# Attention and retention scores on one Trainium2 core: the third part of each score product on 64 or on 128 rows of the array

## The chip, the core and the metric

The kernel runs on one core of one Trainium2 chip. Five engines take part: TensorE (PE in the profile, with its weight loads as PEld), VectorE (DVE), ScalarE (ACT), GpSimd (POOL), and SyncE (SP), which issues the DMAs. Each works through its own queue in order and waits on semaphores for the others. The metric is the device time of one execution in microseconds (us).

## What is computed

A trunk of two layers on 512 tokens of 1024 channels in float32, then a last RMS norm. Each layer normalises x, projects it to all the inputs of three branches, and merges the branches:

```
h = rms_norm(x, norm_g);  proj = h @ w_in
a = diff_attention(aq, ak, av, ...) * silu(az)     # 4 heads, 2 components of 64 dims each
c = short_conv(cx, cb, cc, conv_w) * silu(cz)
r = retention(rq, rk, rv) * silu(rz)               # 4 heads of 64 dims
x = x + (sum_i sigmoid(gate_i) * (branch_i @ w_branch_i)) @ w_out
```

What matters here are the scores. In the attention each head has two components, and for each of them `q @ k.T` over 64 dims, causal, goes through a softmax. In the retention each head has `q @ k.T` over 64 dims with a decay, without a softmax.

## The kernel before

Float32 products are made from parts: a value is split into a high part `hi` (rounded to fp32r) and a low part `lo`, and a product is `hi*hi + hi*lo + lo*hi`. The helper `mm3` issues these three as three products of TensorE. Weights stream in as chunks of 512 KB (`wraw`), which ScalarE casts to `whi` (line 183), and VectorE and GpSimd subtract to `wlo` (line 180), one half of the chunk each. The projections (`proj`) are 24 products of 512 columns, into the PSUM tile `pj`.

Queries and keys have only 64 dims, so two parts fit on the 128 partitions. `queries` makes a tile `st` for each head (or component) `c` with the high part on one half of the partitions (`H[c]`) and the low part on the other. `keys` makes a tile with the key's high part on both halves. One product of the two carries `hi*hi + lo*hi`. The third part is the query's high part times the key's low part. Its operands are the 64 partitions `H[c]` of the query tile and of a tile `lo`, in which the two heads of a pair share the 128 partitions:

```
lo = tr("qk", 10)
for c in range(2):
    V.tensor_tensor(lo[H[c]], y[H[c]], st[H[c]], op=ALU.subtract)
    out.append((st, lo[H[c]]))
```

So each score tile takes two products: one of 128 rows, one of 64 rows. `mm_qk` (line 451) issues them. In an attention step (`attn_step`, one tile of 128 queries against 128, 256, 384 or 512 keys) it has two score tiles, one for each component, and issues the two full-height products first and then the two half-height ones, which lie in different rows of the array. In a retention step (`retention_step`, 128 keys against 512, 384, 256 or 128 queries) there is one score tile, so one full-height and one half-height product. There are 16 steps of each kind in a layer: 64 + 32 products, 192 in both layers.

The order of TensorE's queue is written out by hand. Projections are cut into ticks of 12 products, and `at(lag, fn)` puts a part of a step a few ticks after the part it depends on. Scores are followed by their softmax or mask on VectorE and ScalarE, and the weights (`st`) come back to TensorE as the operands of the value products, some ticks later. The other engines' instructions are put in order by a scheduler when the program is built.

At the start of a layer `Rms.add` squares the eight tiles of x on ScalarE (line 309, tile `sq`, one buffer) and sums them up on GpSimd (line 315, tile `e`). Seven such sums follow one another. Then `Rms.column` sums over the partitions with products on TensorE (line 323), which stand in TensorE's queue between the third and the fourth quarter of the value projection.

Of the kernel before, what the change touches and what calls it, by code (L numbers as in the profile page):

```python
# [10 lines left out]
F32 = mybir.dt.float32  # L11
# [4 lines left out]
PSUM = bass.MemoryType.PSUM  # L16
DRAM = bass.MemoryType.DRAM

P = 128
# [10 lines left out]

# Column offsets of the input projection.
AQ, AK, AV, AZ = 0, 512, 1024, 1536
# [3 lines left out]

# Columns of the small-parameter array.
PG, PCONV, PSUB, PFIN, PW = 0, 16, 40, 42, 50


# [1 line left out]
def merge_chunks(br, jp):  # L42
# [12 lines left out]
def chunk_order(layer):  # L55
    """Chunks of a layer: ("B", col, c) is 512 columns of w_in with K blocks 2c and
    2c+1; ("A", col) 128 columns with all of K; ("W", br, c) 256 columns of
    w_branch; ("O", c) 128 columns of w_out."""
    L = [("B", c, i) for c in (AV, RV) for i in range(4)]
    L += pair_chunks(AK, AQ, AZ)  # L60
    for i in range(4):
        L += conv_chunks(i)
    L += pair_chunks(AK + 256, AQ + 256, AZ + 256)
    for jp in range(4):
        L += merge_chunks(1, jp)
    L += pair_chunks(RK, RQ)
    for jp in range(4):
        L += [("A", RZ + P * jp)] + merge_chunks(0, jp)
    for jp in range(4):
        L += merge_chunks(2, jp)  # L70
    for _ in range(1 if layer < DEPTH - 1 else 2):
        L += [("O", c) for c in range(8)]
    return L


def rot_perm(base):
    """Column order of a rotation head pair block: the two halves of a pair lie
    16 partitions apart within a block of 32."""
    idx = []
    for h in range(4):  # L80
        for ihi in range(2):
            for half in range(2):
                for ilo in range(16):
                    idx.append(base + h * 64 + half * 32 + ihi * 16 + ilo)
    return idx
# [32 lines left out]
def tables():  # L118
    """Rotation tables (attention, then retention k and q of each head pair, the
    decays folded in) and the constant matrices."""  # L120
    f = np.float32
# [33 lines left out]
def tile_hybrid_trunk(ctx: ExitStack, tc: tile.TileContext, xT, w, prm, lam, tab, cmat, outT):  # L155
# [34 lines left out]

# [1 line left out]
    order = [(l, c) for l in range(DEPTH) for c in chunk_order(l)]  # L192
# [21 lines left out]
    def chunk(l, *key):  # L214
        """Next chunk in parts; the one after it is on its way."""
        assert order[pos[0]] == (l, key), (order[pos[0]], l, key)
        while len(parts) < min(LOOK + 1, len(order) - pos[0]):
            split_next()
        pos[0] += 1
        return parts.pop(0)  # L220

# [1 line left out]
    # Projections are cut into ticks of 12 products. The steps of the attentions,  # L223
    # whose products wait for other engines, are placed between them: each part of
    # a step comes a few ticks after the one it depends on.
    now = [0]
# [14 lines left out]

# [1 line left out]
    par = t("par", 1, (P, PW))  # L243
    nc.sync.dma_start(par, prm)
    eps = t("eps", 1, (P, 1))
    G.memset(eps, EPS)
    # The tensor engine comes up to its clock, and the scalar engine's functions
    # load, while the first tiles arrive.
    warm = t("wb", 1, (P, S), mybir.dt.bfloat16)
# [23 lines left out]
    G.memset(ones_d, 1.0 / D)  # L273
    # -lambda of each layer on every partition, and the sub-norm gains.
    nlam, gsub = [], []
# [18 lines left out]
    xsave = dr.tile([D, S], F32, tag="xsave", bufs=1, name="xsave")  # L294

    MASK8 = [i ^ 8 for i in range(32)]
    MASK16 = [i ^ 16 for i in range(32)]

    class Rms:
        """Statistics of the tiles of x over their channels, for tokens q0 to q1."""  # L300

# [3 lines left out]
        def add(self, xk, end=False):  # L305
            """A tile; the end tile's squares stay apart, for a short way to the sums."""
            n = self.n
            sq = t("e2" if self.acc is None else "sq", 1)
            A.activation(sq[:, :n], xk, AF.Square)
            if self.acc is None:  # L310
                self.acc = sq
            elif end:
                self.end = sq
            else:
                G.tensor_tensor(self.acc[:, :n], self.acc[:, :n], sq[:, :n], op=ALU.add)  # L315

        def column(self):
            """1/rms as a column of each token tile."""
            nt = self.n // P
# [11 lines left out]
        def row(self, col):  # L331
            """1/rms as a row on every partition, in PSUM."""
            row = pa()
            for i in range(self.n // P):
                T.transpose(row[:, i * P:(i + 1) * P], col[:, i:i + 1].broadcast_to([P, P]), ident)
            return row

    ctx.enter_context(tc.manual_schedule(engines={mybir.EngineType.PE}))
    for l in range(DEPTH):
        last = l == DEPTH - 1  # L340
        ng = [par[:, PG + 8 * l + k:PG + 8 * l + k + 1] for k in range(NK)]

# [1 line left out]
        xg = {}  # L344
# [8 lines left out]

# [1 line left out]
        def values(col, banks, cs):  # L355
# [34 lines left out]

# [1 line left out]
        h = []  # L392
# [26 lines left out]

        # Queries and keys of two heads (or components) of 64 dims, stacked on the  # L420
        # partitions so that one product carries hi*hi + lo*hi; the third part
        # multiplies the query's hi rows with the key's lo rows.
        H = [slice(0, 64), slice(64, 128)]

        def queries(o, cs, msk):
            y = rotated(o, cs, msk)
            out = []
            for c in range(2):
                st = tr("qk", 10)
                A.copy(st[H[c]], y[H[c]])  # L430
                V.tensor_tensor(st[H[1 - c]], y[H[c]], st[H[c]], op=ALU.subtract)
                out.append((st, st[H[c]]))
            return out

        def keys(o, cs, msk):
            y = rotated(o, cs, msk)
            lo = tr("qk", 10)
            out = []
            for c in range(2):
                st = tr("qk", 10)  # L440
                A.copy(st[H[c]], y[H[c]])
                A.copy(st[H[1 - c]], y[H[c]])
                V.tensor_tensor(lo[H[c]], y[H[c]], st[H[c]], op=ALU.subtract)
                out.append((st, lo[H[c]]))
            return out

        def mm_qk(outs, a, asl, b, bsl):
            """Two of them; their half-height parts lie in different rows of the array."""
            for i in range(2):
                for o, ac, bc in zip(outs, a, b):  # L450
                    T.matmul(o, ac[i][:, asl], bc[i][:, bsl], start=i == 0, stop=i == 1)  # L451
# [5 lines left out]

        # sigmoid(v) = (1 + tanh(v/2)) / 2, which needs no other table than Exp's; the
        # halves are left to later steps.
        def tanh_half(out, o):  # L460
# [11 lines left out]
        def head_out(o, z, g, out):  # L472
            """Normalised, gated head output in parts; o is [v dim, token], z twice the
            gate and g a factor that takes it back."""
            sq = t("sq", 1)
# [19 lines left out]

# [1 line left out]
        rbr, rz = [], {}  # L497
# [19 lines left out]

# [1 line left out]
        cbr = []  # L519
# [18 lines left out]

# [1 line left out]
        abr, az = [], {}  # L540
        cs_a = table(0)

        def attn_qk(p):
            k2 = [keys(proj(AK + 256 * p + P * i), cs_a, MASK8) for i in range(2)]
            q2 = [queries(proj(AQ + 256 * p + P * i), cs_a, MASK8) for i in range(2)]
            return {2 * p + i: (q2[i], k2[i]) for i in range(2)}

        def attn_step(hd, i, o, wt, qk):
            """Scores and weights of one query tile; every second one, the values."""
            q, k = qk[hd]  # L550
# [50 lines left out]

# [1 line left out]
        m = [None] * NK  # L603
# [35 lines left out]
        for jp in range(4):  # L639
            merge(1, cbr, jp, True, False)  # L640
        rk = sum((keys(proj(RK + P * b), table(1 + 2 * b), MASK16) for b in range(2)), [])
        rq = sum((queries(proj(RQ + P * b), table(2 + 2 * b), MASK16) for b in range(2)), [])
# [9 lines left out]

# [1 line left out]
        x2 = []  # L654
# [6 lines left out]
        def out_proj(q0, q1):  # L661
            """The tiles of the output in turn; the last parts of m come late, so that
            the first two tiles' products with them wait behind the others."""
            ws, os = {}, {}
# [70 lines left out]
```

## Time and profile before

| what | value |
|---|---|
| time, median of 3 runs | 1091.72 us (1090.1 to 1093.24) |
| span of the profiled execution, first to last instruction | 1090.5 us |
| TensorE busy | 1078.6 us, 99% of the span, 5010 products |
| VectorE busy | 676.4 us, 62% |
| ScalarE busy | 504.6 us, 46% |
| GpSimd busy | 329.8 us, 30% |
| mean granted TensorE clock | 0.996 |

The profile is of one execution and gives its span; the times of the runs are given apart from it. Products are pipelined, and the time of one in the profile overlaps the next, so a busy share near 100% doesn't say that each product runs at its shortest. What a product costs is better read from the chain of work that ended last: its pieces lie end to end, each as long as the step from one product's end to the next one's. In the chain, a piece such as `PE pa L451 x4` is four products of line 451 into `pa` in a row.

### The profile page before, as it was taken

Reading aid. Unit: us, or ns where it says so; the run is one execution under the profiler, and the core shown is the slowest. Engines: PE = TensorE matmul, PEld = TensorE weight load, DVE = VectorE, ACT = ScalarE, POOL = GpSimd, SP = SyncE. Lnnn points to the kernel's source line nnn. Section 1 sums busy time; section 2 is a strip of 40 time slices with the busy share of each in tenths; the row PEclk is TensorE's granted clock in tenths of the full one; section 3 lists DMA queues with packets and bytes.
Section 4 is the critical chain, followed back from the end, with each engine's and each line's share of the span. In section 5 each row is a group of like instructions: output and inputs, shape, how many; then the busy total and the mean of one; then the engine's idle time right before and its main releaser. Section 6 shows DMA issues by size and latency. Waiting matters only on the chain.

```text
span 1090.5 us, 13839 instructions
## 1 busy us (share of the span) xinstructions
PE 1078.6 (99%) x5010; PEld 878.1 (81%) x5010; DVE 676.4 (62%) x1158; ACT 504.6 (46%) x944; POOL 329.8 (30%) x258
## 2 busy tenths in 40 slices
PE   8999999999999999999999999999999999999997
PEld 6888888888887778888888878888788877788896
DVE  6787686755676556444438766868546946654344
ACT  6454453543554445333444535445344635543343
POOL 6222223221232232323532212232123223232264
PEclk9999999999999999999999999999999999999999
DMA  6322222232234122434422232223212322124353
GB/s 232 117 96 97 78 77 82 94 116 79 77 116 136 58 78 78 135 129 129 158 87 97 86 109 78 78 82 124 85 59 97 135 97 73 62 97 132 111 197 123
DMA packets 34340, 113.64 MB, mean 104 GB/s; under 512 B 3936, under 2 KB 3936, under 8 KB 34272
## 3 DMA queue, kind: packets, MB, share of 16 engines
q1 hardware_dynamic: 34272, 112.76, 30.2%
q8 instruction: 39, 0.64, 0.2%
q14 instruction: 29, 0.24, 0.1%
HBM read 108.55 MB, written 4.19 MB: 103 GB/s over the span
## 4 chain that ended last, share of the span: by engine, by line
PE 97%; POOL 1%; DMA 1%; ACT 0%; DVE 0%; issue 0%; SPq 0%; DVEq 0%; POOLq 0%; ACTq 0%
PE pj L187 29%; PE pj L189 28%; PE pj L188 28%; PE pa L451 3%; PE pa L187 3%; PE pa L188 2%; PE pa L189 2%; PE pa L577 1%; POOL e L315 1%; DMA wraw<-w 1%; PE pa L485 0%; PE pa L484 0%; POOL wlo L180 0%; DVE p L693 0%; PE pa L323 0%
## 5 line engine op out<-in xcount | busy, mean ns | idle before, releaser
L180 POOL TENSOR_TENSOR wlo<-wraw,whi 128x512 fp32r<-128x512 f32 x184 | 252.6, 1375 | 640.4 <-ACT whi L183 619.0
L187 PE MATMUL pj<-h,whi 128*128 128x512 f32 x960 | 384.6, 401 | 0.0
L188 PE MATMUL pj<-h,whi 128*128 128x512 f32 x960 | 375.9, 392 | 0.0
L189 PE MATMUL pj<-h,wlo 128*128 128x512 f32 x960 | 375.7, 391 | 0.0
L183 ACT CAST whi<-wraw 128x512 fp32r<-128x512 f32 x368 | 217.1, 617 | 241.3 <-PE pj L188 178.9
L180 DVE TENSOR_TENSOR wlo<-wraw,whi 128x512 fp32r<-128x512 f32 x184 | 152.9, 832 | 131.7 <-ACT whi L183 128.3
L189 PEld LDWEIGHTS pj<-h,wlo 128*128 128x128 f32 x960 | 180.2, 188 | 41.3
L187 PEld LDWEIGHTS pj<-h,whi 128*128 128x128 f32 x960 | 180.4, 188 | 40.5 <-issue 1.7
L188 PEld LDWEIGHTS pj<-h,whi 128*128 128x128 f32 x960 | 180.6, 188 | 35.2
L187 PE MATMUL pj<-xb,whi 128*128 128x512 f32 x192 | 76.3, 397 | 0.0
L189 PE MATMUL pj<-xb,wlo 128*128 128x512 f32 x192 | 75.3, 392 | 0.0
L188 PE MATMUL pj<-xb,whi 128*128 128x512 f32 x192 | 75.0, 390 | 0.0
L564 ACT ACTIVATE p<-pa,nm 128x128 f32<-128x128 f32 (+3 forms) x64 | 33.4, 525 | 70.5 <-DVE nm L561 70.0
L488 DVE RECIPROCAL e<-e 128x512 f32<-128x512 f32 x16 | 53.6, 3351 | 18.1 <-ACT e L487 18.1
L183 ACT CAST st<-pa 128x256 fp32r<-128x256 f32 (+2 forms) x80 | 29.7, 372 | 74.7 <-DVE pa L506 43.1
L187 PE MATMUL pj<-vm,whi 128*128 128x256 f32 (+1 forms) x192 | 61.0, 318 | 0.0
L189 PE MATMUL pj<-vm,wlo 128*128 128x256 f32 (+1 forms) x192 | 60.7, 316 | 0.0
L188 PE MATMUL pj<-vm,whi 128*128 128x256 f32 (+1 forms) x192 | 60.6, 316 | 0.0
L621 DVE SCALAR_TENSOR_TENSOR wb<-wa,pj 128x512 f32<-128x512 f32 x32 | 22.0, 688 | 44.9 <-PE pj L189 44.9
L451 PE MATMUL pa<-qk 128*128 128x256 f32 (+3 forms) x192 | 46.5, 360 | 0.0
L451 PEld LDWEIGHTS pa<-qk 128*128 128x128 f32 x192 | 29.8, 185 | 19.1 <-issue 13.6
L180 DVE TENSOR_TENSOR st<-pa,st 128x256 fp32r<-128x256 f32 (+2 forms) x80 | 33.7, 421 | 18.4 <-ACT st L183 18.2
(123 smaller groups left out, 1414.7 us busy)
## 6 DMA issues: line engine op xcount, KB each, us to landing
wraw<-w SPq DMA_DIRECT2D x183, 512.0 KB, 3.3
tab<-tab SPq DMA_DIRECT2D x10, 512.0 KB, 3.3
xm<-xT SPq DMA_DIRECT2D x16, 256.0 KB, 3.5
xsave<-xm SPq DMA_DIRECT2D x8, 256.0 KB, 2.0
xm<-xsave SPq DMA_DIRECT2D x8, 256.0 KB, 2.7
outT<-p SPq DMA_DIRECT2D x8, 256.0 KB, 2.1
wraw<-w SPq DMA_DIRECT2D x2, 256.0 KB, 3.1
cm<-cmat SPq DMA_DIRECT2D x1, 256.0 KB, 6.6
```

The lines of the kernel that those rows point to most:

```text
L180: eng.tensor_tensor(lo, x, hi, op=ALU.subtract)
L183: A.copy(hi, x)
L187: T.matmul(out, wh, xh, start=start, stop=False)
L188: T.matmul(out, wh, xl, start=False, stop=False)
L189: T.matmul(out, wl, xh, start=False, stop=stop)
L315: G.tensor_tensor(self.acc[:, :n], self.acc[:, :n], sq[:, :n], op=ALU.add)
L451: T.matmul(o, ac[i][:, asl], bc[i][:, bsl], start=i == 0, stop=i == 1)
L488: V.reciprocal(r, r)
L564: A.activation(pc[:, :n], sp[:, :n], AF.Exp, bias=nm, scale=0.125, accum_out=sm)
L577: T.transpose(tp[:, j * P:(j + 1) * P], p1[:, j * P:(j + 1) * P], ident)
L621: V.scalar_tensor_tensor(y, g, 1.0, o, op0=ALU.add, op1=ALU.mult)
```

## The change

The low part of the keys gets four tiles of its own, `klo`, made once, one for each head of the two pairs. In each, one half of the partitions is set to zero by GpSimd at the start and never written again. `keys` writes the low part into the other half, the half `H[c]` on which the query tile has its high part. `queries` and `keys` hand out whole tiles, so the third part is a product of 128 rows whose other half is multiplied by zero. `mm_qk` issues the two products of one score tile one after the other, instead of both first parts and then both third parts. The tag `qk` has 8 buffers instead of 10. (Comments in the file are gone too, and line numbers behind the new lines are shifted: line 451 becomes 453, line 315 becomes 321, line 323 becomes 329.)

```diff
+    H = [slice(0, 64), slice(64, 128)]
+    klo = [tr("klo", 4) for _ in range(4)]
+    for n, lo in enumerate(klo):
+        G.memset(lo[H[1 - n % 2]].bitcast(F32), 0.0)
...
-                st = tr("qk", 10)
+                st = tr("qk", 8)
                 A.copy(st[H[c]], y[H[c]])
                 V.tensor_tensor(st[H[1 - c]], y[H[c]], st[H[c]], op=ALU.subtract)
-                out.append((st, st[H[c]]))
+                out.append((st, st))
...
-        def keys(o, cs, msk):
+        def keys(o, cs, msk, i):
             y = rotated(o, cs, msk)
-            lo = tr("qk", 10)
             out = []
             for c in range(2):
-                st = tr("qk", 10)
+                st, lo = tr("qk", 8), klo[2 * i + c]
                 A.copy(st[H[c]], y[H[c]])
                 A.copy(st[H[1 - c]], y[H[c]])
                 V.tensor_tensor(lo[H[c]], y[H[c]], st[H[c]], op=ALU.subtract)
-                out.append((st, lo[H[c]]))
+                out.append((st, lo))
             return out
 
         def mm_qk(outs, a, asl, b, bsl):
-            """Two of them; their half-height parts lie in different rows of the array."""
-            for i in range(2):
-                for o, ac, bc in zip(outs, a, b):
+            for o, ac, bc in zip(outs, a, b):
+                for i in range(2):
                     T.matmul(o, ac[i][:, asl], bc[i][:, bsl], start=i == 0, stop=i == 1)
...
-            k2 = [keys(proj(AK + 256 * p + P * i), cs_a, MASK8) for i in range(2)]
+            k2 = [keys(proj(AK + 256 * p + P * i), cs_a, MASK8, i) for i in range(2)]
...
-        rk = sum((keys(proj(RK + P * b), table(1 + 2 * b), MASK16) for b in range(2)), [])
+        rk = sum((keys(proj(RK + P * b), table(1 + 2 * b), MASK16, b) for b in range(2)), [])
```

TensorE's queue at the first attention step, before (`pa<-qk` is a score product, `pj<-h,whi` a product of a projection; the size is that of the output):

```order
L188 MATMUL pj<-h,whi 128x512
L189 MATMUL pj<-h,wlo 128x512
L451 MATMUL pa<-qk 128x128 x4
L187 MATMUL pj<-h,whi 128x512
L188 MATMUL pj<-h,whi 128x512
L189 MATMUL pj<-h,wlo 128x512
```

and after:

```order
L188 MATMUL pj<-h,whi 128x512
L189 MATMUL pj<-h,wlo 128x512
L453 MATMUL pa<-qk 128x128
L453 MATMUL pa<-klo,qk 128x128
L453 MATMUL pa<-qk 128x128
L453 MATMUL pa<-klo,qk 128x128
L187 MATMUL pj<-h,whi 128x512
L188 MATMUL pj<-h,whi 128x512
```

The four products of the step stand at the same place between the same projections; the two third parts, now with `klo`, no longer stand side by side.

GpSimd's queue at the start, before (`wlo` is the low part of a weight chunk, `e` the running sum of squares of x, `wu` two zero columns of the convolution):

```order
L273 MEMSET ones_d 128x1
L526 MEMSET wu 128x2
L180 ISA
L180 TENSOR_TENSOR wlo<-wraw,whi 128x512
L315 TENSOR_TENSOR e_222<-e_222,sq 128x512
L180 TENSOR_TENSOR wlo<-wraw,whi 128x512
L315 TENSOR_TENSOR e_222<-e_222,sq 128x512 x2
L180 TENSOR_TENSOR wlo<-wraw,whi 128x512
L315 TENSOR_TENSOR e_222<-e_222,sq 128x512 x4
L180 TENSOR_TENSOR wlo<-wraw,whi 128x512 x16
```

and after:

```order
L273 MEMSET ones_d 128x1
L300 MEMSET klo 64x512 x4
L528 MEMSET wu 128x2
L180 ISA
L180 TENSOR_TENSOR wlo<-wraw,whi 128x512 x2
L321 TENSOR_TENSOR e_230<-e_230,sq 128x512 x2
L180 TENSOR_TENSOR wlo<-wraw,whi 128x512
L321 TENSOR_TENSOR e_230<-e_230,sq 128x512 x5
L180 TENSOR_TENSOR wlo<-wraw,whi 128x512 x16
```

Four memsets of `klo` are new, and the first sum of squares has moved behind the low part of the second weight chunk. In the rest of TensorE's queue nothing moves, and on the other engines a few casts and subtractions change places with a neighbour.

## Rows read from the trace of the kernel before

**Rows 1.** The page's head: the span.

```profile
span 1090.5 us, 13839 instructions
```

**Rows 2.** The page's chain that ended last: shares by engine.

```profile
PE 97%; POOL 1%; DMA 1%; ACT 0%; DVE 0%; issue 0%; SPq 0%; DVEq 0%; POOLq 0%; ACTq 0%
```

**Rows 3.** Waits of PE, longest (who <- whom: us, times, longest).

```profile
PE pa L323 <- POOL e L315: 2.5, 1, 2.5
```

**Rows 4.** PE's waits again, of its weight loads: the longest.

```profile
PEld pa L451 <- issue: 13.6, 48, 0.4
```

**Rows 5.** The chain in pieces (start us, length us, what): attention score groups.

```profile
88.91 0.43 PE pa L451 x4
89.33 0.43 PE pj L187
...
97.80 0.55 PE pa L451 x4
...
106.92 0.72 PE pa L451 x4
...
116.34 0.88 PE pa L451 x4
117.22 0.32 PE pa L187
```

**Rows 6.** The chain in pieces: retention score groups.

```profile
337.43 0.65 PE pa L451 x2
338.08 0.43 PE pj L187
...
341.01 0.54 PE pa L451 x2
...
347.94 0.43 PE pa L451 x2
348.36 0.37 PE pa L187
...
351.82 0.31 PE pa L451 x2
```

**Rows 7.** The chain in pieces: full-height products of 512, 256, 128 and 384 columns.

```profile
88.67 0.23 PE pj L189
...
117.54 0.12 PE pa L188
...
130.11 0.44 PE pa L577 x4
...
348.73 0.17 PE pa L188
348.91 0.18 PE pa L189
```

**Rows 8.** POOL in order of time, start (start us, us, line, op, [idle before <-releaser]).

```profile
0.77 0.52 POOL L250 MEMSET wb<- 128x512 bf16 x1
...
6.92 1.30 POOL L180 TENSOR_TENSOR wlo<-wraw,whi 128x512 fp32r<-128x512 f32 x1 [5.56 <-ACT whi L183]
8.17 1.74 POOL L315 TENSOR_TENSOR e<-e,sq 128x512 f32<-128x512 f32 x1
10.60 1.62 POOL L180 TENSOR_TENSOR wlo<-wraw,whi 128x512 fp32r<-128x512 f32 x1 [0.69 <-ACT whi L183]
```

**Rows 9.** The chain in pieces: the last two sums of squares.

```profile
22.13 1.28 POOL e L315
...
24.15 1.29 POOL e L315
```

**Rows 10.** PE by stretch (from:to us, length, busy (products), PEclk, DMA share, GB/s).

```profile
27.40:30.70 3.30, 3.30 (x9) 0.50 0.60 190
```

**Rows 11.** VectorE and PE in order of time at retention's last step.

```profile
420.34 0.28 DVE L180 TENSOR_TENSOR st<-pa,st 128x128 fp32r<-128x128 f32 x1
...
423.05 0.22 PE L187 MATMUL pa<-st,vm 128*128 128x128 f32 x1
```

More of the change, by code (lines that the diff above doesn't have):

```diff
@@ L418, in rotated @@
             return t1
-        H = [slice(0, 64), slice(64, 128)]
         def queries(o, cs, msk):
```

## The prediction

> **What bounds the kernel now.** I read the chain of work that ended last first, then who waited for whom on PE, then the chain piece by piece around the score products. The chain is PE for 97% of a span of 1090.5 us [rows 1, 2]: whatever PE spends on a product is spent on the end time, and whatever another engine spends is free as long as PE does not come to wait for it. PE waits in one place that matters, 2.5 us for POOL's line 315 near the start [rows 3]. So two questions remain: what the 192 score products cost PE in its own queue, and whether the change moves that one wait.
>
> The pieces of the chain lie end to end, so they can be added. A product of 512 columns takes 0.23 us, one of 384 columns 0.17 to 0.18 (0.175 below), one of 256 columns 0.12, and four of 128 columns 0.44, so 0.11 each [rows 7]. All of these use 128 rows. The score groups are dearer, and so is the product that follows them: it takes 0.43 where 0.23 is normal [rows 5, 6]. A group costs its own piece plus the next product's excess over its normal price.
>
> **What the score groups cost today.** Attention, four products per step, two of them of half height: 128 columns 0.43 + 0.43 - 0.23 = 0.63 us; 256 columns 0.55 + 0.20 = 0.75; 384 columns 0.72 + 0.20 = 0.92; 512 columns 0.88, and the product behind it has 256 columns and takes 0.32 instead of 0.12, so 1.08 [rows 5, 7]. Retention, two products per step, one of half height: 512 columns 0.65 + 0.20 = 0.85; 384 columns 0.54 + 0.20 = 0.74; 256 columns 0.43, and the product behind it (384 columns) takes 0.37 instead of 0.175, so 0.625; 128 columns 0.31 + 0.20 = 0.51 [rows 6, 7]. Each of these eight stands eight times in the trace (four heads, two layers); the first stands in the rows, with one 0.43 of the product behind for all.
>
> Take the full-height products off at their normal price and the half-height part remains. At 512 columns it is 1.08 - 0.46 = 0.62 in attention, where there are two half-height products, and 0.85 - 0.23 = 0.62 in retention, where there is one. At 384 columns 0.57 and 0.565, at 256 columns 0.51 and 0.505, at 128 columns 0.41 and 0.40. So two facts are in the rows. The second half-height product of a pair is free: the pair does run side by side. And going to half height and back costs 0.3 to 0.4 us over a product's normal price, every time, with or without a partner. The weight loads of these groups show it too: PE's loader stands idle ahead of them 48 times, 13.6 us in all, with nothing that it waits for [rows 4].
>
> **The change part by part.**
>
> *Half height to full height.* Attention now pays four normal products, retention two. I price them by [rows 7], where full-height products of each width stand between others with no gap. Attention: 0.63 - 0.44 = 0.19; 0.75 - 0.48 = 0.27; 0.92 - 0.70 = 0.22; 1.08 - 0.92 = 0.16; together 0.84, eight times: 6.7 us saved. Retention: 0.85 - 0.46 = 0.39; 0.74 - 0.35 = 0.39; 0.625 - 0.24 = 0.385; 0.51 - 0.22 = 0.29; together 1.46, eight times: 11.7 us saved. Sum: **-18.4 us**, all on PE and so all on the path. Both ends: the gap could go wholly (-18.4) or stay wholly (rival one). I take the first, because no full-height neighbour shows a gap: the four products at 130.11 are narrow, stand alone between 512-column ones, and cost 0.44 [rows 7].
>
> The Trainium skill bears on this from both sides. "TensorEngine Tiling (Array Packing)", section Theoretical Speedup, gives up to 2x for a contraction of 64 rows or fewer, which speaks against this change; its section Key Properties says that a change of tiling mode drains the engine, which speaks for it. The trace agrees with the first only where two half-height products stand together, as 0.62 against 0.62 shows, and has 0.3 to 0.4 us for the second. By the first rule alone the change would lose time (rival one gives that sum); by both it gains what the rows say.
>
> *The order inside a group.* The two products of one score tile now follow each other into the same PSUM bank. The three products of every projection already do that at 0.23 us each. Nothing.
>
> *Four key tiles with a zero half.* POOL gets four memsets of 64x512 near the start. The nearest row is its memset of 128x512 bf16, 0.52 us; as many bytes in one of the new ones, twice that if the 4-byte words count double: 2.1 to 4.2 us for four. POOL is idle for 5.56 us between its last small memset and its first weight part [rows 8]. Hidden; without that cover up to 4.2 us would come ahead of the first weight part. The subtractions into these tiles keep their number and size, and each tile is reused in the same turn as the shared one was.
>
> *POOL's order at the start.* The built order moves something that the diff doesn't mention. Before, the first sum of squares (line 315, at 8.17) runs ahead of the second chunk's weight part, which waits for its data until 10.60 [rows 8]. After, it stands behind that weight part and starts at about 10.60 + 1.62 = 12.2, where the second sum ran before. Every later sum then comes one round later, since each waits for a square that ScalarE writes only when the sum before has read the one buffer. A round is 24.15 - 22.13 = 2.02 us, and the last sum, which ends at 24.15 + 1.29 = 25.44, is what PE waits for [rows 3, 9]. PE's next instruction in its queue is the product with these sums, so all projections behind it wait too: **+2.0 us**, uncovered.
>
> *The clock behind that stall.* After the stall of before, the granted clock stood at 0.50 (the lower level, 1.2 GHz) from 27.4 to 30.7, and PE started 9 products there [rows 10]; at 0.23 each they would be 2.1 us instead of 3.3 to 3.8. PE had stood idle in the stall before the clock fell. A longer stall may bring a second such stretch, up to 1.7 us more; it may also put part of the slow stretch into the stall, a gain of up to 1.7. I take 0 and keep the loss for the range.
>
> *Sum.* 1090.5 - 18.4 + 2.0 = 1074.1 us for the span. The median of the runs, 1091.7, lies 1.2 above the profiled span; with that, **1075.3 us**.
>
> **The rivals.**
>
> *One: the gap isn't the height's.* If the 0.3 to 0.4 us belonged to something that stays (entering the score group, its PSUM banks, the release of its tiles), the change would only give up the free partner: one more product per attention step, (0.11 + 0.12 + 0.175 + 0.23) x 8 = 5.1 us, plus the 2.0 of the start: **1098.8 us**, slower. For it: nothing in the trace shows the same tiles at full height. Against it: the transposes also write a fresh PSUM tile and have no gap [rows 7]. The gaps are 18.4 + 5.1 = 23.5 us in all; the sign turns where less than 7.1 of them go, 30%.
>
> *Two: another engine takes the gain back.* With PE faster, a product may come to wait for VectorE or ScalarE. The tightest step that I found is the last one of retention: VectorE ends the low part at 420.34 + 0.28 = 420.62, and the value products that take it begin on PE at 423.05 [rows 11], 2.4 us to spare; PE loses at most two score groups of 0.39 between such a pair. So I expect no wait. If retention were paced by VectorE after all, its 11.7 us would stay: **1087.0 us**.
>
> *Three: half the gap stays*, for instance on the way into a group but not on the way out: 18.4 - 11.75 = 6.7 gained, less 2.0: **1087.0 us** as well.
>
> **How the numbers follow.** Forecast 0.84; rival one 0.05; rivals two and three together 0.08; no difference, where the gains of three are smaller still and the start costs both terms, 0.03. Two and three count as faster, and 0.3% is 3.3 us, about what a measurement of this kernel can tell from no change. So faster 0.92, same 0.03, slower 0.05. The range: below, no cost at the start, or a shorter slow stretch, with the spread of the runs (1.6 us below the median), 1091.7 - 18.4 - 1.6 = 1071.7; above, the second slow stretch and the runs' 1.5 above the median, 1075.3 + 1.7 + 1.5 = 1078.5, and a microsecond for narrow products that cost more between other neighbours, 1079.5. That leaves out less than 2 in 10.
>
> **What would show it.** In the chain of after: a four-product group of 128 columns at about 0.44, of 512 columns at 0.92, a retention pair of 512 columns at 0.46, and the product behind each back at 0.23 to 0.28. PE's wait for line 321 (315 before) at 4.5 us, ending near 27.5. One slow stretch of the clock behind it, or two. Wrong would be: groups whose piece keeps 0.2 us or more over these prices; a new wait of PE for VectorE in retention; a stall at the start that is no longer than 2.5 us.

## The result and the profile after

The kernel after takes 1076.52 us (median of 4 runs, 1075.94 to 1077.81), the kernel before 1091.94 us: the ratio is 0.9855, 95% interval 0.9843 to 0.9868, about 15.4 us faster. The forecast was 1075.3. The execution that was profiled is the slowest of the four (1077.81 us; its span, which leaves out 1.8 us, is 1076.0), and the lines of after in this section are of that one.

The head of the page of after, and its TensorE clock in 40 slices:

```profile
span 1076.0 us, 13845 instructions
...
PEclk9899999999999999999999999999999999999998
```

The chain is still PE for 97%. What changed is seen in its pieces (start us, length us, what), for the same steps as [rows 5] and [rows 6]. Attention, four products each:

```profile
92.53 0.40 PE pa L453 x4
92.93 0.28 PE pj L187
...
101.23 0.47 PE pa L453 x4
...
110.08 0.69 PE pa L453 x4
...
119.27 0.94 PE pa L453 x4
120.20 0.12 PE pa L187
```

Retention, two products each:

```profile
337.65 0.46 PE pa L453 x2
338.10 0.23 PE pj L187
...
340.87 0.35 PE pa L453 x2
...
347.43 0.23 PE pa L453 x2
347.66 0.18 PE pa L187
...
350.95 0.17 PE pa L453 x2
351.13 0.28 PE pj L187
```

The product behind a group is back at its normal price: 0.23 for 512 columns, 0.12 for 256, 0.18 for 384, where [rows 5, 6] had 0.43, 0.32 and 0.37. Only behind a 128-column group does it take 0.28, and the group is shorter by nearly as much: 0.40 + 0.28 - 0.23 = 0.45 in attention, 0.17 + 0.28 - 0.23 = 0.22 in retention. The idle time of the weight loads in front of the score products [rows 4] no longer stands in the list of waits at all.

Where the rest went is read from PE's wait for the sums of squares, and from the granted clock behind it (PE by stretch: from:to, length, busy (products), PEclk, DMA share, GB/s):

```profile
PE pa L329 <- POOL e L321: 4.4, 1, 4.4
```

```profile
27.80:34.60 6.80, 6.80 (x20) 0.50 0.61 183
```

The wait was 2.5 us before [rows 3], and the clock stood at its lower level (0.50, 1.2 GHz) for some 3.4 us [rows 10]; now it stands there for 6.8.

The two traces can be set against each other at three places. Two of them are the four transposes of the start and the second product behind the last score group, in the chain of before:

```profile
33.70 0.44 PE pa L335 x4
...
951.89 0.24 PE pj L188
...
1083.70 0.42 PE pa L335 x2
```

and in the chain of after:

```profile
37.33 0.44 PE pa L341 x4
...
937.07 0.23 PE pj L188
...
1068.87 0.68 PE pa L341 x2
```

The first stands 3.6 us later than before: so much was lost at the start. The second stands 14.8 ahead, so 18.4 us were gained between the two places, where all score groups lie. The third place is the end, 14.4 ahead (1090.46 and 1076.03, less rounded): another 0.4 went in the last stretch. So -18.4 + 3.6 + 0.4 = -14.4 us, the difference of the two spans.

The third line of each chain shows most of that last loss: the two transposes of the end begin 14.8 ahead as well, and take 0.68 where they took 0.42. In after the clock had fallen just before them, in before it had not yet (PE by stretch, first before, then after):

```profile
1080.00:1085.40 5.40, 2.55 (x21) 1.00 0.00 0
```

```profile
1068.90:1075.90 7.00, 0.63 (x2) 0.50 0.41 151
```

### The profile page after: what moved, and what is told of

Its sections match the earlier page's. It is cut to its first block, busy times and chain, and to the rows that moved or that the text cites. A ratio compares the mean times of both kernels' runs of the same rounds, so it can differ in the third digit from the quotient of the medians.

```text
span 1076.0 us, 13845 instructions
## 1 busy us (share of the span) xinstructions
PE 1062.3 (99%) x5010; PEld 883.2 (82%) x5010; DVE 680.7 (63%) x1158; ACT 504.4 (47%) x944; POOL 331.6 (31%) x262
## 4 chain that ended last, share of the span: by engine, by line
PE 97%; POOL 1%; DMA 1%; ACT 0%; DVE 0%; issue 0%; SPq 0%; DVEq 0%; POOLq 0%; ACTq 0%
PE pj L187 29%; PE pj L189 28%; PE pj L188 28%; PE pa L453 3%; PE pa L189 2%; PE pa L188 2%; PE pa L187 2%; POOL e L321 1%; PE pa L579 1%; DMA wraw<-w 1%; PE pa L487 0%; PE pa L486 0%; POOL wlo L180 0%; PE pa L329 0%; DVE p L695 0%
## 5 line engine op out<-in xcount | busy, mean ns | idle before, releaser
L180 DVE TENSOR_TENSOR wlo<-wraw,whi 128x512 fp32r<-128x512 f32 x184 | 156.3, 850 | 125.0 <-ACT whi L183 121.5
L189 PEld LDWEIGHTS pj<-xb,wlo 128*128 128x128 f32 x192 | 36.0, 188 | 8.4
L188 PEld LDWEIGHTS pj<-xb,whi 128*128 128x128 f32 x192 | 36.1, 188 | 7.9
```

Of the source, the lines that this page charges most:

```text
L180: eng.tensor_tensor(lo, x, hi, op=ALU.subtract)
L188: T.matmul(out, wh, xl, start=False, stop=False)
L189: T.matmul(out, wl, xh, start=False, stop=stop)
```

## The experiments

**The order alone.** The kernel before, with only the two loops of `mm_qk` changed over:

```diff
-            for i in range(2):
-                for o, ac, bc in zip(outs, a, b):
+            for o, ac, bc in zip(outs, a, b):
+                for i in range(2):
```

> The kernel before with the order of after alone: each score tile's full-height product is followed at once by its own half-height one, all third parts still on 64 rows. Theory (each change of height costs 0.3 to 0.4 us, a second half-height product beside the first is free): an attention step now changes height twice, so it pays its half-height part twice: (0.62 + 0.57 + 0.51 + 0.41) x 8 = 16.9 us more than before, about 1108.8 us against 1091.9; an attention group of 512 columns about 1.7 us in the chain instead of 1.08; retention unchanged. Rival one (the gap belongs to the score group and not to the height): only the free partner is lost, 5.1 us, about 1097.

Measured: 1109.68 us (1108.94 to 1110.61) against 1092.4 on the same chip, ratio 1.0154 (1.0137 to 1.0170): 17.3 us slower, where the theory wanted 16.9 and the rival 5.1. The chain of this run, the first four attention steps:

```profile
89.08 0.82 PE pa L451 x4
89.91 0.43 PE pj L187
...
98.36 1.05 PE pa L451 x4
99.41 0.43 PE pj L187
...
107.98 1.28 PE pa L451 x4
109.25 0.43 PE pj L187
...
117.94 1.52 PE pa L451 x4
119.46 0.31 PE pa L187
```

The 512-column step costs 1.52 + 0.31 - 0.12 = 1.71, where it cost 1.08: the half-height part of 0.62 is paid twice. In the program only this order differs, so half the change alone would have made the kernel slower by more than the whole change gains.

**The height alone.** The kernel after, with the loops of before (both first parts, then both third parts):

```diff
-            for o, ac, bc in zip(outs, a, b):
-                for i in range(2):
+            for i in range(2):
+                for o, ac, bc in zip(outs, a, b):
```

> The kernel after with the order of before: both first parts, then both third parts, all on 128 rows. Theory (height alone decides): the same as after, 1076.5 within 1 us, groups at 0.44 to 0.92 us. Rival (two products in a row into the same PSUM tile are what saves the time in attention): attention's 6.7 us come back, about 1083.

Measured: 1076.56 us (1076.14 to 1076.74), the same as after. At full height the order inside a group is worth nothing that these runs can tell; two products in a row into one PSUM tile neither cost nor save.

**The pair twice.** The kernel before, with the two half-height products of an attention step issued a second time behind the first two:

```diff
-                    T.matmul(o, ac[i][:, asl], bc[i][:, bsl], start=i == 0, stop=i == 1)
+                    T.matmul(o, ac[i][:, asl], bc[i][:, bsl], start=i == 0, stop=i == 1 and len(outs) == 1)
+            if len(outs) == 2:
+                for o, ac, bc in zip(outs, a, b):
+                    T.matmul(o, ac[1][:, asl], bc[1][:, bsl], start=False, stop=True)
```

> The kernel before, with the pair of half-height products of each attention step issued twice in a row (the third part is added twice, so the scores are not the reference's). Theory (the cost is in the change of height, not in the product): the second pair costs one product's normal price per step, (0.11 + 0.12 + 0.175 + 0.23) x 8 = 5.1 us, about 1097.0 against 1091.9. Rival (each half-height product or pair carries the 0.3 to 0.4 us itself): 2.11 x 8 = 16.9 us, about 1108.8.

Measured: 1097.37 us (1095.48 to 1098.90) against 1092.4, ratio 1.0043 (1.0031 to 1.0055): 5.0 us, as the theory had it. In the chain the second pair has a piece of its own (line 454):

```profile
89.06 0.43 PE pa L451 x4
89.49 0.11 PE pa L454 x2
89.61 0.43 PE pj L187
...
98.06 0.55 PE pa L451 x4
98.61 0.12 PE pa L454 x2
...
107.31 0.72 PE pa L451 x4
108.03 0.18 PE pa L454 x2
...
116.90 0.89 PE pa L451 x4
117.80 0.23 PE pa L454 x2
```

Two half-height products together take 0.11, 0.12, 0.18 and 0.23, what one full-height product of that width takes [rows 7]. The pair does run side by side at no extra cost; the 0.3 to 0.4 us belong to going in and out, and are paid once whether one product, one pair or two pairs stand between. What they are made of inside the engine, no run here separates.

**Retention alone.** The kernel after, with attention's third part on the halves of the new tiles and its loops as before:

```diff
-                out.append((st, st))
+                out.append((st, st, st[H[c]]))
...
-                out.append((st, lo))
+                out.append((st, lo, lo[H[c]]))
...
-            for o, ac, bc in zip(outs, a, b):
-                for i in range(2):
-                    T.matmul(o, ac[i][:, asl], bc[i][:, bsl], start=i == 0, stop=i == 1)
+            for i in range(2):
+                for o, ac, bc in zip(outs, a, b):
+                    j = 2 if i == 1 and len(outs) == 2 else i
+                    T.matmul(o, ac[j][:, asl], bc[j][:, bsl], start=i == 0, stop=i == 1)
```

> Only retention on 128 rows; attention's third parts stay on 64 rows, side by side, as before, reading the halves of the new tiles. POOL's order at the start is that of after. Theory (a height change costs the same with one half-height product as with two): retention's 11.7 us are gained and the start costs 2.0 to 3.6, so about 1082 to 1084 against 1091.9. Rival (the cost goes with the number of half-height products, of which retention has 64 of 192 score products' 96 third parts, a third): 23.5 / 3 less retention's own slots, about 6 us gained at most, 1088 to 1090.

Measured: 1083.73 us (1083.33 to 1084.05) against 1092.4, ratio 0.9916 (0.9901 to 0.9930): 8.7 us faster, which is 11.7 less 3.0 for the start; in the chain of this run the four transposes of the start stand at 36.80, 3.1 later than before. Attention then brings 1083.73 - 1076.56 = 7.2, where 6.7 was forecast. Retention, with one third of the score products, brings most of the gain, because its half-height product had no partner.

**The start: the memsets on VectorE.**

```diff
-        G.memset(lo[H[1 - n % 2]].bitcast(F32), 0.0)
+        V.memset(lo[H[1 - n % 2]].bitcast(F32), 0.0)
```

> The kernel after with the four memsets on VectorE instead of GpSimd; with that the built order of GpSimd's and ScalarE's start is that of before again (the first sum of squares ahead of the second chunk's weight part). Theory (the moved sum costs one round of 2.0 us of stall and up to one slow stretch of the clock, 1.6): 2.0 to 3.6 us less than after, 1073 to 1074.5 against 1076.5; PE's wait for the sums back from 4.4 to 2.5 us, one slow stretch of 3.4 us. Rival (the start is hidden behind something later): 1076.5.

Measured: 1073.78 us (1072.15 to 1074.05), ratio to before 0.9822 (0.9809 to 0.9836), beside the kernel after itself on the same chip:

> The kernel after once more, beside the two on the same chip: 1076.5 within 1 us, both theories.

which took 1076.49 us (1075.12 to 1076.78), ratio 0.9848 (0.9834 to 0.9861). So 2.7 us are back, the clock's part included. GpSimd's order is that of before, and PE's wait is 2.0 us, near the 2.5 of before. The profiled execution shows one thing more. It took 1072.15 us, the shortest of its four runs, and in it the clock never fell at the start (the wait, then PE by stretch):

```profile
PE pa L329 <- POOL e L321: 2.0, 1, 2.0
```

```profile
23.00:25.30 2.30, 0.35 (x2) 1.00 0.00 0
25.40:27.30 1.90, 1.90 (x13) 1.00 0.04 9
27.40:30.70 3.30, 3.30 (x17) 1.00 0.61 179
```

17 products start between 27.4 and 30.7 where [rows 10] has 9. The three other runs of the same kernel took 1073.6 to 1074.05. One stretch at the lower level is worth about 8 products x 0.2 = 1.6 us, which is also the distance of this run to the others; their traces were not taken, so that they had such a stretch is inferred. Their mean granted clocks agree with it: 0.996, 0.995 and 0.995 against 0.998, and 3.4 us at half the clock are 0.0016 of the span.

**The start: two tiles for the squares.** As above, and the squares alternate between `sq` and `wc`:

```diff
-            sq = t("e2" if self.acc is None else "sq", 1)
+            self.i += 1
+            sq = t("e2" if self.acc is None else ("sq", "wc")[self.i % 2], 1)
```

> The same, and the squares of x alternate between two tiles (the convolution's tile wc is the second), so that a square needn't wait for the sum before it. Theory (the round of 2.0 us is the two engines waiting for each other through one buffer): seven sums of 1.3 to 1.7 us with two weight parts between them end by about 22 to 23 us, where PE is still busy until 23; no wait of PE for the sums, no slow stretch, another 2.5 + 1.6 us gained, 1069 to 1070.5. Rival (the scaled tiles of x, which now stand behind squares on ScalarE, come late for PE instead): a new wait of PE of 1 to 3 us near the start, 1072 to 1074.

Measured: 1073.73 us (1073.09 to 1074.01), the same as with the memsets on VectorE alone. The theory failed, and the rival was right on the time and on a new wait of 1 to 3 us. It had half of the cause: PE no longer waits for the sums, but for VectorE's low part of the next weight chunk, not for a scaled tile of x. The chain of this run leads from that low part back through VectorE to a scaled tile that ScalarE makes late, behind a square (first the wait, then the chain):

```profile
PE pj L188 <- DVE wlo L180: 2.0, 1, 2.0
```

```profile
20.12 0.49 ACT sq L316
...
20.94 0.63 ACT xb L356
...
21.60 1.78 DVE xb L357
...
25.64 0.61 DVE wlo L180
```

The clock falls behind this stall as it did behind the other (PE by stretch):

```profile
27.10:30.40 3.30, 3.30 (x9) 0.50 0.75 205
```

**The start: four tiles for the squares.** With the memsets on VectorE, and the squares in the four tiles of `ez`:

```diff
-            sq = t("e2" if self.acc is None else "sq", 1)
+            sq = t("e2", 1) if self.acc is None else t("ez", 4)
```

> As the run with two square tiles, but the squares rotate through the four tiles of the tag ez (gates of heads, unused at the start), so that ScalarE doesn't stand still before a square and the scaled tiles of x behind it come early too. Theory (the start's stall is the engines waiting for each other through too few square tiles, first at the sums, then, with two tiles, at VectorE's low part of the last weight chunk, because ScalarE's scaled tiles of x came late): no wait of PE between 6 and 34 us above 0.5, no slow stretch, 2.0 to 2.5 + up to 1.6 us less than with the memsets on VectorE alone, 1069.5 to 1072 against 1073.8. Rival (GpSimd's sums and VectorE's subtractions slow one another and the last low part stays late): a wait of 1 to 2 us at the same place, 1073 to 1074.

Measured: 1071.98 us (1071.39 to 1073.66) against 1093.35 in that call, ratio 0.9814 (0.9800 to 0.9828), the best median of the study, but its interval overlaps those of the two runs before it (0.9809 and 0.9810 to 0.9836). The first line below is PE's wait, the next two are pieces of the chain behind it, the others VectorE in order of time:

```profile
PE pj L188 <- DVE wlo L180: 1.4, 1, 1.4
```

```profile
27.35 0.23 PE pj L189
...
30.75 0.23 PE pj L189
```

```profile
17.31 1.78 DVE L356 SCALAR_TENSOR_TENSOR xb<-xm,par,xb 128x512 fp32r<-128x512 f32 x1
...
24.52 0.74 DVE L356 SCALAR_TENSOR_TENSOR xb<-xm,par,xb 128x512 fp32r<-128x512 f32 x1
...
25.43 0.68 DVE L180 TENSOR_TENSOR wlo<-wraw,whi 128x512 fp32r<-128x512 f32 x1
```

The same operation takes 1.78 us at 17.31, while GpSimd makes a weight part and adds squares, and 0.74 at 24.52, where GpSimd stands idle from 24.58 on. VectorE reaches the low part that PE waits for only at 25.43. PE's products behind the wait stay at 0.23 us, so the clock did not fall in this execution. The theory's "no wait above 0.5" failed and the rival holds in part: the wait shrank from 2.0 to 1.4, and didn't go. That GpSimd's work is what slows VectorE is read from one trace side by side; no run separated it. What might remove the wait (VectorE's lambda work out of the start, or less on GpSimd) wasn't tried.

By the clocks on record, most of the lead in the median is the clock's. Three of the five runs have a mean granted clock of 0.997 to 0.998 and took 1071.4 to 1072.0; the other two (0.995, 0.996) took 1073.3 and 1073.7. With the memsets alone only one run of four had 0.998. Among runs of like clock, four square tiles are about half a microsecond ahead, which is little beside the spread. Why the clock fell less often is not shown.

## Why the prediction was right

*The score groups, -18.4 us.* Right in sum and in its parts. The chain of after has nearly the prices that were taken: 0.45, 0.47, 0.69 and 0.94 in attention against 0.44, 0.48, 0.70 and 0.92, and 0.46, 0.35, 0.23 and 0.22 in retention against 0.46, 0.35, 0.24 and 0.22. Between the two marks 18.4 us were gained. That the gap goes with the change of height, which the trace of before only suggested, is shown by the first and the third experiment: one more change of height per attention step costs 17.3 us, one more pair without a change costs 5.0.

*Rival one* (the gap belongs to the score group) falls with the same two runs, and with the second: the same groups, tiles and order at full height have no gap. The Trainium skill's page "TensorEngine Tiling (Array Packing)" gives both halves of this in its sections Theoretical Speedup and Key Properties: up to two products of 64 rows in the time of one, and a drain of the engine at a change of mode. The traces agree with the first, with 0.23 us for a pair of 512 columns; for the second they show a cost, 0.3 to 0.4 us for going in and out, and not the drain itself. That the second outweighs the first here is this kernel's: only one pair, or one product, stood between two changes.

*The four memsets, hidden.* Right: they took 2.2 us together, near the lower bound, in GpSimd's idle stretch, of which 3.2 us are left.

*The moved sum, +2.0 us.* Right: the wait grew from 2.5 to 4.4, and undoing GpSimd's order gave 2.7 back, the clock's part included. Reading the built order, not the diff, brought this term.

*The clock, taken at 0.* This is the term that was mis-sized. Of the 3.6 us lost at the start 2.0 are the moved sum, and 1.6 the lower level, which held for 6.8 us instead of 3.4; that is within the bound of 1.7 that was kept for the range. In the second trace of the same kernel the four transposes stand at 36.67, with PE's wait ending at 27.24, and the clock cost 1.2: there the fall came inside the stall, as the prediction had thought possible. The 0.4 of the last stretch was no term of the sum; 0.26 of it is the clock again, at the two last transposes.

*The total, and some luck.* Span against span, the sum gave 1074.1 and the profiled execution took 1076.0: 1.9 short, which is the clock at the start and the last stretch. The times lie nearer, 1075.3 and 1076.5. The prediction added the 1.2 us by which the median of before lay above its profiled span; the median of after lies only 0.5 above its own, since the slowest of the four executions was profiled. So about 0.7 us of the agreement comes from which executions were profiled, and is no merit of the sum.

*Rivals two and three.* No new wait of PE in retention or attention stands in the list of waits, and no part of the gap stayed.

## What to carry to other kernels

Putting two half-height products side by side saved one product's time here; entering and leaving half height costs 0.3 us (128 columns) to 0.4 us (256 and more). An estimate from these prices, which no run set against full height: side by side pays from two pairs of 512 columns, or three or four of fewer columns, between two changes. A lone half-height product between full-height ones lost 0.29 to 0.39 us here: there, pad the other half with zeros. And a few small instructions on an engine that looks idle may change the built order of that engine, so compare the orders before the times.

## What the runs showed of the hardware that was not expected

The granted clock at the start is not a fixed price of a stall. After a wait of 2.5 us it stood low for 3.4 us [rows 3, 10], after one of 4.4 us for 6.8. After one of 2.0 us (memsets on VectorE) and one of 1.4 us (four square tiles) it did not fall at all in the profiled executions, though another wait of 2.0 us, with two square tiles, did bring it down, for 3.3 us at least.

Nor does the fall always come behind the stall. In the run with the height alone PE waited 4.1 us, until 27.03, and the clock was down before that: a mean of 0.77 over 4.4 us makes 2.0 us at the lower level, and only the last 0.3 of the stretch lie behind the wait (PE by stretch):

```profile
22.90:27.30 4.40, 0.32 (x3) 0.77 0.00 0
```

What of the low stretch lies inside the wait costs nothing. From the first product with the sums to the four transposes PE took 6.6 us where the clock did not fall (25.38 to 31.99, memsets on VectorE), 8.2 in before, 9.9 in after, 9.1 in this run and 9.4 in the second trace of after. So the clock near the start cost from 0 to 3.3 us on top of the stall. The runs of one kernel spread by as much, with the clock: beside the first four experiments before took 1090.75 us at a mean granted clock of 0.997 and 1094.33 at 0.994.
